# Transposing by VectorE blocks and a round trip through DRAM in place of TensorE, in a two-layer hybrid network

## The chip, the cores and the metric

The kernel runs on one core of a Trainium2 chip. The metric is the device time of one execution in microseconds (us). A core has five engines with a program each: TensorE (PE in the rows, its weight loads PEld), VectorE (DVE), ScalarE (ACT), GpSimd (POOL) and SyncE (SP). They run side by side and wait for one another by semaphores; each takes its instructions in the order in which they stand. TensorE ran at the full granted clock, 1.00 (2.4 GHz), throughout the profiled execution.

## The reference

Sequence of 256 tokens, width 2048, two layers, everything float32. Cut to what matters:

```
layer 0: x = x + dilated_attention(x)   # 16 heads of 128; q, k RMS-normed; softmax over three patterns; @ w_o
         x = x + conv_ffn(x)            # (silu(conv(h @ w_up)[gate]) * conv(..)[up]) @ w_down, inner width 5632
layer 1: x = x + mlstm_mixer(x)         # 4 heads, q/k of 256, v and output gate of 512; gated scan; @ w_out
         x = x + conv_ffn(x)
```

## The kernel before

Every product with a weight matrix is float32 made from two float32r parts. ACT copies a piece of a weight tile to the high part `wh` (L105), DVE subtracts to get the low part `wl` (L107). Activations have a high and a low half too (`xs`, `HID`). Three products are summed: high x high, high x low weight, low activation x high weight.

All weight tiles run through one list of *parts* of at most 1024 columns. A loop at the end of the kernel takes part j: it loads and splits it (`load_split`), and emits the products of part j - 2 (`AHEAD = 2`). Buffers: four for `wst` (the raw tile), three each for `wh` and `wl`. Work that belongs between parts is hung up with `at(j, f)`, to stand just ahead of the products of part j, or is called from the last part's `post`. The tile framework then orders each engine's program and sets the semaphores; it may move such work back when it reckons its inputs to come late.

Two kinds of product:

- *stationary-x* (`mm_b`): 128 tokens of x are stationary, 512 weight columns stream. Used for query, key and value, and for the mixer's value and output gate. A chunk of 512 output columns has eight parts of 12 matmuls. In the first four parts of the program `late=True` puts all products with `wl` last; otherwise, for each weight row block, high, low and low-activation products alternate (L207, L208, L209).
- *stationary-w* (`mm_t`): 128 weight columns are stationary, the 512 columns [high | low] of the activation stream. `wide` is the product with `wh`, `narrow` the one with `wl` (256 columns). Used for the FFN, both output projections and the mixer's query and key.

The attention comes first: eight chunks q, k, q, k, ... of four heads, and then four chunks of values. Of a chunk come the RMS norm of each head (`qk_post`: squares on ACT, the power -0.5 on POOL at L149, scaling on DVE at L310), and then transposes on TensorE, which bring [token, channel] to [channel, token] in PSUM, copied out by ACT (`qk_transpose`, L320 and L324). Scores, softmax (`scores`) and the transposes of the probabilities (`p_transpose`, L355 and L357) follow, one head a part. `pv` multiplies with the values. In the mixer, the gated output of a head is transposed in the same way (`hs_transpose`, L661), and `gate_weights` spreads the running maximum of the gates over partitions with a float32 matmul (L574).

Of the kernel before, what the change touches and what calls it, by code (L numbers as in the profile page):

```python
# [9 lines left out]
F32 = mybir.dt.float32  # L10
# [62 lines left out]
def hybrid_kernel(ctx: ExitStack, tc: tile.TileContext, x, small, negT, sel, g_attn, gain, w_qkv, w_o, w_gates, w_qk, w_vo,  # L73
# [6 lines left out]
    work = ctx.enter_context(tc.tile_pool(name="work", bufs=2))  # L80
    psum = ctx.enter_context(tc.tile_pool(name="psum", bufs=4, space=PSUM))


# [89 lines left out]

    def mm_t(acc, wh, wl, base, ks, xs, first, last):
# [13 lines left out]

        for step in ((narrow, wide) if last else (wide, narrow)):
            step()  # L190

    def mm_b(accs, wh, wl, ks, xs, first, last, n=512, late=False):

        if late:
            order = [(xp, wp, i, tt) for xp, wp in ((0, wh), (S, wh), (0, wl)) for i in range(len(ks)) for tt in range(NT)]
            for xp, w, i, tt in order:
                nc.tensor.matmul(accs[tt], xs[ks[i]][:, xp + tt * P:xp + (tt + 1) * P], w[:, i * n:(i + 1) * n],
                                 start=first and xp == 0 and w is wh and i == 0, stop=False)
            return
        for i, k in enumerate(ks):  # L200
            h = wh[:, i * n:(i + 1) * n]
            lo = wl[:, i * n:(i + 1) * n]
            for tt in range(NT):
                xh = xs[k][:, tt * P:(tt + 1) * P]
                xl = xs[k][:, S + tt * P:S + (tt + 1) * P]
                a = accs[tt]
                nc.tensor.matmul(a, xh, h, start=first and i == 0, stop=False)  # L207
                nc.tensor.matmul(a, xh, lo, start=False, stop=False)  # L208
                nc.tensor.matmul(a, xl, h, start=False, stop=last and i == len(ks) - 1)  # L209

# [35 lines left out]


    st = {}

# [23 lines left out]

    def b_chunk(src, xs_of, post, opening=False):

        hold = {}

        def mm(wh, wl, q):
            if q == 0:
                hold["a"] = [acc_tile(f"accb{tt}") for tt in range(NT)]  # L280
            mm_b(hold["a"], wh, wl, (2 * q, 2 * q + 1), xs_of(), q == 0, q == 7, late=opening and q < 4)
# [31 lines left out]

    def qk_transpose(which, g):
        raw = st.pop(("raw", which, g))
        for a in range(0, GRP, 2):
            pt = psum.tile([P, 512], F32, name="ptq", tag="m")
            for b in range(2):
                for tt in range(NT):
                    nc.tensor.transpose(pt[:, b * S + tt * P:b * S + (tt + 1) * P],  # L320
                                        raw[:, tt, (a + b) * P:(a + b + 1) * P], ident)
            slot = ((0, 1, 20), (2, 3, 21))[which][(g * 2 + a // 2) % 3]
            t = work.tile([P, 512], F32, name=f"qkT{which}", tag=f"hid{slot}", bufs=1)
            nc.scalar.activation(t, pt, AF.Copy, scale=C("qk_gain")[:, which:which + 1])  # L324
            for b in range(2):
                qkT[which, g * GRP + a + b] = t[:, b * S:(b + 1) * S]
# [23 lines left out]

    def p_transpose(h):
        p = SMX.pop(h)
        pp = psum.tile([P, 512], F32, name="ppt", tag="m")
        for b in range(3):
            nc.tensor.transpose(pp[:, b * P:(b + 1) * P], p[:, b * P:(b + 1) * P], ident)  # L355
# [19 lines left out]
    def pv(h):  # L375
        v = st["v", h // GRP]
        a = (h % GRP) * P
        t = PT.pop(h)
        po = psum.tile([P, 512], F32, name="po", tag="m")
        nc.tensor.matmul(po[:, :P], v[:, 0, a:a + P], t[:, :P], start=True, stop=True)  # L380
        nc.tensor.matmul(po[:, P:S], v[:, 0, a:a + P], t[:, P:S], start=True, stop=False)  # L381
        nc.tensor.matmul(po[:, P:S], v[:, 1, a:a + P], t[:, S:384], start=False, stop=True)  # L382
# [7 lines left out]
    def attn_units():  # L390
        for c in range(8):
            g, which = c // 2, c % 2
            post = qk_post(which, g)
            if c == 0:

                j = b_chunk([w_qkv[c, q] for q in range(4)], lambda: st["xs"], lambda accs: st.update(first=accs),
                            opening=True)
                at(12, lambda post=post: post(st.pop("first")))
                at(j + 9, lambda: qk_transpose(0, 0))
# [107 lines left out]
    def gate_product():  # L507
        xs = st["xs"]
        pg = psum.tile([P, 512], F32, name="pg", tag="m")
        for k in range(KT):  # L510
            nc.tensor.matmul(pg[:16], st["gw"][:, k], xs[k], start=k == 0, stop=k == KT - 1)  # L511
        st["sel"] = work.tile([P, LH * P], F32, name="sel", tag="hid21", bufs=1)
        nc.sync.dma_start(st["sel"], sel)
        st["negT"] = work.tile([P, 384], F32, name="negT", tag="hid20", bufs=1)
# [53 lines left out]

    def gate_weights():
        (F, c), M = st["gF"], st["gM"]  # L570
        args = []
        for h in range(LH):
            pm = psum.tile([P, 512], F32, name="pm", tag="m")
            nc.tensor.matmul(pm[:, :S], st["sel"][:LH, h * P:(h + 1) * P], M, start=True, stop=True)  # L574
            ar = work.tile([P, 384], F32, name=f"ar{h}", tag=f"hid{16 + h}", bufs=1)
            nc.vector.tensor_tensor(ar[:, :S], pm[:, :S], st["negT"][:, :S], op=ALU.add)
            nc.vector.tensor_tensor(ar[:, S:], pm[:, P:S], st["negT"][:, S:], op=ALU.add)
            for tt, sl in ((0, slice(0, S)), (1, slice(S, 384))):
                nc.scalar.activation(ar[:, sl], ar[:, sl], AF.Exp, bias=c[:, tt, h:h + 1])
            args.append(ar)  # L580
        pmc = psum.tile([P, 512], F32, name="pmc", tag="m")
# [4 lines left out]
        nc.scalar.activation(en, en, AF.Exp, scale=-1.0)  # L586
        st["E"], st["en"] = args, en

# [67 lines left out]
    def hs_transpose(h):  # L656
        o = st.pop(("hs", h))
        for a in range(4):
# [6 lines left out]
            HID[4 * h + a] = t  # L665

    def lstm_units():
        for n in range(KT):
            which, h, i = n // 8, (n % 8) // 2, n % 2

            def post(acc, n=n, which=which, h=h, i=i):
# [3 lines left out]
                LQ[which, h, i] = t  # L675
            side = {0: gate_product, 2: gate_logs, 4: gate_sums, 6: gate_max, 9: gate_weights}.get(n)

# [5 lines left out]
        for h in range(LH):  # L683
# [4 lines left out]
            if h < LH - 1:  # L688
                at(j + 2, lambda h=h: hs_transpose(h))

# [107 lines left out]
```

## Time and profile before

| | us |
|---|---|
| median of 3 runs (lowest, highest) | 2257.88 (2257.12, 2258.18) |
| profiled execution: its own time | 2257.33 |
| its span on the core | 2255.5 |
| TensorE busy in the span | 2249.5 |
| VectorE busy | 1572.6 |
| ScalarE busy | 1224.4 |
| GpSimd busy | 20.1 |

The times of the rows are those of the profiled execution. A matmul's row gives its duration with fill and drain, so durations of neighbours overlap; what a matmul costs on TensorE is the distance between starts. DVE and ACT instructions overlap a little at their starts as well. In a group row, what follows the bar is busy time in total, mean duration in ns, then the engine's idle time just ahead and what ended it.

### The profile page before, as it was taken

To read this page: it belongs to the slowest core of one execution; us is meant where nothing else is said; L and a number is where in the kernel's file an instruction comes from. 1 tells how busy PE (TensorE), PEld (TensorE's weight loads), DVE (VectorE), ACT (ScalarE), POOL (GpSimd) and SP (SyncE) were. 2 spreads that over 40 slices of the span, in tenths; PEclk is the share of its full clock that TensorE was granted. 3 is DMA by queue.
4 is the path that set the end of the run, shared out by engine and by line. 5 is a ranking of instruction groups with operands and counts; after the bars stand their busy time and mean duration, and the time that the engine had idled before them with its cause. 6 is when DMAs were issued, how large, how long until landed. Compare 5 with 4: busy or idle time off the path is not lost.

```text
span 2255.5 us, 31873 instructions
## 1 busy us (share of the span) xinstructions
PE 2249.5 (100%) x12370; PEld 1948.0 (86%) x12370; DVE 1572.6 (70%) x2522; ACT 1224.4 (54%) x1878; POOL 20.1 (1%) x20
## 2 busy tenths in 40 slices
PE   9999999999999999999999999999999999999999
PEld 7888888888888888888888887888888888888888
DVE  6666566777865688876677555667888656788755
ACT  6666445555644555565556444456665445566543
POOL 0000000000000000000000000000000000000000
PEclk9999999999999999999999999999999999999999
DMA  7544445555545655545555454455554556555464
GB/s 296 181 168 168 166 171 187 187 188 189 191 162 191 219 187 187 188 164 188 208 177 187 173 182 176 174 190 186 193 192 176 169 191 213 189 191 192 166 202 144
DMA packets 67399, 419.90 MB, mean 186 GB/s; under 512 B 7600, under 2 KB 9904, under 8 KB 28592
## 3 DMA queue, kind: packets, MB, share of 16 engines
q1 hardware_dynamic: 64800, 415.76, 52.7%
q8 instruction: 97, 1.59, 0.3%
q10 hardware_dynamic: 2448, 2.11, 0.3%
q14 instruction: 54, 0.44, 0.1%
HBM read 415.74 MB, written 2.10 MB: 185 GB/s over the span
## 4 chain that ended last, share of the span: by engine, by line
PE 99%; DVE 0%; DMA 0%; issue 0%; ACT 0%; SPq 0%; DVEq 0%; ACTq 0%
PE acct L181 51%; PE acct L186 26%; PE accb L208 6%; PE accb L209 6%; PE accb L207 6%; PE pn L611 0%; PE ptq L320 0%; PE psc L332 0%; DMA wst<-in_w_qkv 0%; PE ppt L355 0%; PE pg L511 0%; PE po L381 0%; PE po L382 0%; PE po L380 0%; PE psc L331 0%; PE pth L661 0%
## 5 line engine op out<-in xcount | busy, mean ns | idle before, releaser
L107 DVE TENSOR_TENSOR wl<-wst,wh 128x1024 fp32r<-128x1024 f32 (+1 forms) x864 | 972.1, 1126 | 327.6 <-ACT wh L105 315.7
L105 ACT ACTIVATE wh<-wst 128x1024 fp32r<-128x1024 f32 (+1 forms) x864 | 844.3, 977 | 552.2 <-PE acct L181 342.8
L181 PE MATMUL acct<-xs,wh 128*128 128x512 f32 x3072 | 736.7, 391 | 0.0
L181 PEld LDWEIGHTS acct<-xs,wh 128*128 128x128 f32 x3072 | 563.9, 188 | 109.4 <-issue 0.3
L181 PE MATMUL acct<-hid,wh 128*128 128x512 f32 x1920 | 483.9, 394 | 0.0
L186 PEld LDWEIGHTS acct<-xs,wl 128*128 128x128 f32 x3072 | 393.9, 191 | 15.0
L181 PEld LDWEIGHTS acct<-hid,wh 128*128 128x128 f32 x1920 | 344.2, 188 | 64.8
L186 PE MATMUL acct<-xs,wl 128*128 128x256 f32 x3072 | 398.5, 283 | 0.0
L186 PEld LDWEIGHTS acct<-hid,wl 128*128 128x128 f32 x1920 | 256.8, 188 | 21.2 <-ACT hid L384 0.2
L186 PE MATMUL acct<-hid,wl 128*128 128x256 f32 x1920 | 261.5, 279 | 0.0
L207 PE MATMUL accb<-wh,xs 128*128 128x512 f32 x624 | 249.7, 400 | 0.1
L208 PE MATMUL accb<-wl,xs 128*128 128x512 f32 x624 | 243.4, 390 | 0.5 <-DVE wl L107 0.5
L209 PE MATMUL accb<-wh,xs 128*128 128x512 f32 x624 | 243.5, 390 | 0.0
L209 PEld LDWEIGHTS accb<-wh,xs 128*128 128x128 f32 x624 | 117.1, 188 | 24.9
L208 PEld LDWEIGHTS accb<-wl,xs 128*128 128x128 f32 x624 | 117.3, 188 | 24.1 <-DVE wl L107 1.0
L207 PEld LDWEIGHTS accb<-wh,xs 128*128 128x128 f32 x624 | 117.2, 188 | 23.6 <-ACT wh L105 0.6
L474 ACT ACTIVATE hid<-pr 128x256 fp32r<-128x256 f32 x88 | 36.7, 418 | 176.2 <-DVE pr L472 176.2
L240 DVE TENSOR_TENSOR uz<-acct,ev 128x256 f32<-128x256 f32 x88 | 37.4, 425 | 123.6 <-ACT ev L238 123.6
L238 ACT ACTIVATE ev<-acct 128x256 f32<-128x256 f32 x192 | 73.8, 385 | 75.8 <-PE acct L181 66.5
L468 ACT ACTIVATE sg<-gy 128x256 f32<-128x256 f32 x88 | 36.8, 418 | 142.3 <-DVE gy L456 142.3
L456 DVE SCALAR_TENSOR_TENSOR gy<-gz,sm,gy 128x255 f32<-128x255 f32 (+2 forms) x224 | 106.7, 478 | 2.3 <-ACT gy L452 1.7
L244 DVE TENSOR_TENSOR xT<-acct,xT 128x256 f32<-128x256 f32 x96 | 40.8, 425 | 96.4 <-PE acct L181 96.1
(144 smaller groups left out, 998.9 us busy)
## 6 DMA issues: line engine op xcount, KB each, us to landing
wst<-in_w_up SPq DMA_DIRECT2D x176, 1024.0 KB, 4.8
wst<-in_w_down SPq DMA_DIRECT2D x128, 704.0 KB, 4.1
wst<-in_w_qkv SPq DMA_DIRECT2D x46, 1024.0 KB, 4.8
wst<-in_w_vo SPq DMA_DIRECT2D x32, 1024.0 KB, 4.8
wst<-in_w_o SPq DMA_DIRECT2D x16, 1024.0 KB, 4.7
wst<-in_w_qk SPq DMA_DIRECT2D x16, 1024.0 KB, 4.8
wst<-in_w_out SPq DMA_DIRECT2D x16, 1024.0 KB, 4.7
xT<-in_x SPq DMA_DIRECT2D x8, 256.0 KB, 8.2
```

The costliest lines, as they stand in the source:

```text
L105: nc.scalar.activation(wh[:, :n], w, AF.Copy)
L107: nc.vector.tensor_tensor(wl[:, :n], w, wh[:, :n].bitcast(F32), op=ALU.subtract)
L181: nc.tensor.matmul(acc, wh[:, (base + i) * P:(base + i + 1) * P], xs[k], start=first and i == 0, stop=last and i == n - 1)
L186: nc.tensor.matmul(acc[:, :S], wl[:, (base + i) * P:(base + i + 1) * P], xs[k][:, :S], start=False, stop=False)
L207: nc.tensor.matmul(a, xh, h, start=first and i == 0, stop=False)
L208: nc.tensor.matmul(a, xh, lo, start=False, stop=False)
L209: nc.tensor.matmul(a, xl, h, start=False, stop=last and i == len(ks) - 1)
L238: nc.scalar.activation(t, acc[:, S:], AF.Copy)
L240: nc.vector.tensor_tensor(z, acc[:, :S], t, op=ALU.add)
L244: nc.vector.tensor_tensor(xT[k], acc[:, :S], xT[k], op=ALU.add)
L456: nc.vector.scalar_tensor_tensor(y[:, d:], z[:, :S - d], w, y[:, d:], op0=ALU.mult, op1=ALU.add)
L468: nc.scalar.activation(g, y, AF.Silu)
```

## The change

1. The transposes of query, key and probabilities, and of three of the four mixer heads, leave TensorE. DVE transposes blocks of 32x32 in place of that (`turn_blocks`), four transfers on POOL's queue write the four partition groups into a DRAM tile, each so that the block column becomes the partition, and one more fetches it back (`fetch_blocks`). ACT (and DVE for the mixer's low half) then reads the fetched tile where it read PSUM. A probability tile is fetched straight into `PT`.
2. The work is hung up at other parts: a chunk is turned 4 parts behind its end and taken 5 parts later; scores come at j + 10, 12, 14, 16 (before j + 7 to 10) and the probabilities' turns 4 parts behind each.
3. `mm_b` always has the products with `wl` last.
4. The second of four parts in the down projection has `narrow` ahead of `wide` (`turn`).
5. `gate_weights` works with two float32r halves of the maximum, one head in each of four units, and `sel` is loaded by POOL with a cast.

```diff
-    def mm_b(accs, wh, wl, ks, xs, first, last, n=512, late=False):
...
+    def mm_b(accs, wh, wl, ks, xs, first, last, n=512):
+
+        for xp, w in ((0, wh), (S, wh), (0, wl)):
+            for i, k in enumerate(ks):
+                for tt in range(NT):
+                    nc.tensor.matmul(accs[tt], xs[k][:, xp + tt * P:xp + (tt + 1) * P], w[:, i * n:(i + 1) * n],
...
+    def turn_blocks(srcs, tag, bufs):
...
+        t = work.tile([P, 4, m, n, 32], F32, name="tb", tag=tag, bufs=bufs)
+        for u, src in enumerate(srcs):
+            nc.vector.transpose(t[:, :, :, u].rearrange("p j m r -> p m j r"),
+                                src.rearrange("p (m j r) -> p m j r", m=m, j=4))
+        d = dram.tile([4, 32, 4, run], F32, name=f"d{run}", tag=f"d{run}")
+        for i in range(4):
+            nc.gpsimd.dma_start(d[:, :, i].rearrange("j c x -> c j x"),
+                                t[32 * i:32 * (i + 1)].rearrange("p j m n r -> p j (m n r)"))
+        return d
+
+    def fetch_blocks(d, dst):
+        nc.gpsimd.dma_start(dst, d.rearrange("j c i x -> (j c) (i x)"))
...
-        for step in ((narrow, wide) if last else (wide, narrow)):
+        for step in ((narrow, wide) if last or turn else (wide, narrow)):
...
+    def qk_turn(which, g):
+        raw = st.pop(("raw", which, g))
+        d = turn_blocks([raw[:, tt] for tt in range(NT)], "tok", 4)
+        t = work.tile([P, 1024], F32, name="td", tag="tok", bufs=4)
+        fetch_blocks(d, t)
+        st["td", which, g] = t
...
+    def p_turn(h):
+        d = turn_blocks([SMX.pop(h)], "y", 3)
         t = work.tile([P, 384], F32, name=f"PT{h}", tag=f"hid{h + 4}", bufs=1)
-        nc.scalar.activation(t, pp[:, :384], AF.Copy)
-        PT[h] = t
+        fetch_blocks(d, t)
...
-                at(j + 5, lambda which=which, g=g: qk_transpose(which, g))
+                at(j + 4, lambda which=which, g=g: qk_turn(which, g))
+                at(j + 9, lambda which=which, g=g: qk_take(which, g))
             if which == 1:
                 for a in range(GRP):
-                    at(j + 7 + a, lambda h=g * GRP + a: scores(h))
-                    at(j + 11 + a, lambda h=g * GRP + a: p_transpose(h))
+                    at(j + 10 + 2 * a, lambda h=g * GRP + a: scores(h))
+                    at(j + 14 + 2 * a, lambda h=g * GRP + a: p_turn(h))
...
+        for i in range(2):
+            nc.tensor.matmul(pm[:, :S], st["sel"][:LH, h * P:(h + 1) * P], m2[:, i], start=i == 0, stop=i == 1)
...
-                at(j + 2, lambda h=h: hs_transpose(h))
+                at(j + 2, lambda h=h: hs_turn(h))
+                at(j + 7, lambda h=h: hs_take(h))
```

TensorE's order at the scores of the third head group, before (`psc` are scores, `accb` the running chunk, `ptq` and `ppt` transposes; this is the fourth score of the group):

```order
L207 MATMUL accb1_1713<-wh_1591,xs1_97 128x512
L208 MATMUL accb1_1713<-wl_1593,xs1_97 128x512
L209 MATMUL accb1_1713<-wh_1591,xs1_97 128x512
L331 MATMUL psc_1730<-qkT1_1559,qkT0_1376 128x128
L332 MATMUL psc_1730<-qkT1_1559,qkT0_1376 128x256
L207 MATMUL accb0_1712<-wh_1626,xs2_107 128x512
L208 MATMUL accb0_1712<-wl_1628,xs2_107 128x512
```

and now, three scores of that group (the first was named for 4.7 parts earlier):

```order
L199 MATMUL accb0_1681<-wh_1748,xs11_200 128x512
L199 MATMUL accb1_1682<-wh_1748,xs11_200 128x512
L346 MATMUL psc_1699<-qkT1_1677,qkT0_1481 128x128
L347 MATMUL psc_1699<-qkT1_1677,qkT0_1481 128x256
L346 MATMUL psc_1752<-qkT1_1677,qkT0_1481 128x128
L347 MATMUL psc_1752<-qkT1_1677,qkT0_1481 128x256
L346 MATMUL psc_1824<-qkT1_1679,qkT0_1483 128x128
L347 MATMUL psc_1824<-qkT1_1679,qkT0_1483 128x256
L199 MATMUL accb0_1681<-wl_1750,xs10_197 128x512
```

Scores that stood one a part stand three in a row, inside a part.

VectorE's order in the same place, before (from the second head's maxima to the next `wl`; 12 rows stand between two of them at most):

```order
L340 TENSOR_REDUCE mx_1635<-sc_1633 128x1 x2
L341 TENSOR_SCALAR mx_1635<-mx_1635 128x2
L334 TENSOR_TENSOR sc_1696<-psc_1693,sm_68 128x384
L344 SCALAR_TENSOR_TENSOR p_1638,den_1636<-e_1637,sm_68 128x128
L340 TENSOR_REDUCE mx_1698<-sc_1696 128x1 x2
L344 SCALAR_TENSOR_TENSOR p_1638,den_1636<-e_1637,sm_68 128x256
L341 TENSOR_SCALAR mx_1698<-mx_1698 128x2
L346 RECIPROCAL den_1636<-den_1636 128x2
L348 TENSOR_SCALAR p_1638<-p_1638,den_1636 128x128
L348 TENSOR_SCALAR p_1638<-p_1638,den_1636 128x256
L107 TENSOR_TENSOR wl_1691<-wst_1687,wh_1689 128x1024
```

and now, the last rows of 26 between two low parts (`tb` is the block-transposed tile):

```order
L248 STREAM_TRANSPOSE tb_1771<-raw_1647 128x4x4x32
L359 SCALAR_TENSOR_TENSOR p_1760,den_1758<-e_1759,sm_70 128x128
L248 STREAM_TRANSPOSE tb_1771<-raw_1647 128x4x4x32
L359 SCALAR_TENSOR_TENSOR p_1760,den_1758<-e_1759,sm_70 128x256
L248 STREAM_TRANSPOSE tb_1815<-p_1707 128x3x4x32
L361 RECIPROCAL den_1758<-den_1758 128x2
L355 TENSOR_REDUCE mx_1829<-sc_1827 128x1
L363 TENSOR_SCALAR p_1760<-p_1760,den_1758 128x128
L363 TENSOR_SCALAR p_1760<-p_1760,den_1758 128x256
L355 TENSOR_REDUCE mx_1829<-sc_1827 128x1
L108 TENSOR_TENSOR wl_1859<-wst_1855,wh_1857 128x1024
```

The next low part now stands behind two heads, the scaling of a query chunk and three block transposes.

GpSimd's order over the attention, before, is powers alone:

```order
L149 ISA
L149 TENSOR_TENSOR rcol<-ir,mhalf 128x4
L149 TENSOR_TENSOR qf<-ir,mhalf 128x8 x8
L149 TENSOR_TENSOR rcol<-ir,mhalf 128x4 x2
L149 TENSOR_TENSOR lf_11863<-ir,mhalf 128x2
```

and now, from the power of a key chunk to that of the next query chunk (`d` are DRAM tiles, `td` and `PT` fetched ones):

```order
L150 TENSOR_TENSOR qf_1463<-ir_1464,mhalf_72 128x8
L252 DMA d96_1505<-tb_1503 32x4x96 x2
L257 DMA PT5_1417<-d96_1412 128x384
L252 DMA d96_1505<-tb_1503 32x4x96 x2
L252 DMA d96_1548<-tb_1546 32x4x96 x2
L257 DMA PT6_1510<-d96_1505 128x384
L252 DMA d96_1548<-tb_1546 32x4x96 x2
L252 DMA d256_1558<-tb_1555 32x4x256 x2
L257 DMA PT7_1553<-d96_1548 128x384
L252 DMA d256_1558<-tb_1555 32x4x256 x2
L257 DMA td_1563<-d256_1558 128x1024
L150 TENSOR_TENSOR qf_1658<-ir_1659,mhalf_72 128x8
```

A fetch waits for its four writes, and what stands behind it on the queue waits with it, the next power included.

## Rows read from the trace of the kernel before

**Rows 1.** The page, engines: busy us (share of span) x instructions.
```profile
PE 2249.5 (100%) x12370; PEld 1948.0 (86%) x12370; DVE 1572.6 (70%) x2522; ACT 1224.4 (54%) x1878; POOL 20.1 (1%) x20
```
**Rows 2.** The page, chain that ended last, share by engine.
```profile
PE 99%; DVE 0%; DMA 0%; issue 0%; ACT 0%; SPq 0%; DVEq 0%; ACTq 0%
```
**Rows 3.** PE timeline at a query chunk's transposes: start us, duration us, instruction.
```profile
114.03 0.39 PE L209 MATMUL accb<-wh,xs 128*128 128x512 f32 x1
114.26 1.03 PE L320 MATMUL ptq<-sm,raw 128*128 128x128 f32 x8
...
115.36 0.39 PE L208 MATMUL accb<-wl,xs 128*128 128x512 f32 x1
```
**Rows 4.** PE timeline at a probability tile's transposes.
```profile
133.97 0.40 PE L209 MATMUL accb<-wh,xs 128*128 128x512 f32 x1
134.21 0.49 PE L355 MATMUL ppt<-sm,p 128*128 128x128 f32 x3
...
134.78 0.39 PE L208 MATMUL accb<-wl,xs 128*128 128x512 f32 x1
```
**Rows 5.** Windows, one head group: all engines; then DVE at L107, at L310.
```profile
71.50:121.00 49.50, 49.50 (x237) 41.31 (x237) 31.98 (x79) 31.12 (x69) 3.28 (x2) 1.00 0.50 170
...
71.50:121.00 49.50, 19.44 (x16) 1.00 0.50 170
...
71.50:121.00 49.50, 3.32 (x16) 1.00 0.50 170
```
**Rows 6.** Groups of instructions: the three kinds of transposes on PE.
```profile
L320 PE MATMUL ptq<-sm,raw 128*128 128x128 f32 x64 | 8.3, 272 | 0.0
...
L355 PE MATMUL ppt<-sm,p 128*128 128x128 f32 x48 | 7.8, 272 | 0.0
...
L661 PE MATMUL pth<-sm,osb 128*128 128x128 f32 x32 | 4.1, 272 | 0.0
```
**Rows 7.** PE timeline at the float32 gate matmuls, and a row of 256-column passes.
```profile
1193.42 1.99 PE L574 MATMUL pm<-cm,sel 4*128 4x256 f32 x8
1195.34 0.50 PE L181 MATMUL acct<-xs,wh 128*128 128x512 f32 x1
...
1197.68 1.60 PE L186 MATMUL acct<-xs,wl 128*128 128x256 f32 x12
```
**Rows 8.** PE timeline near the start.
```profile
20.15 0.50 PE L208 MATMUL accb<-wl,xs 128*128 128x512 f32 x1 [0.53 <-DVE wl L107]
```
**Rows 9.** Waits: us in total, times, longest us.
```profile
ACT wh L105 <- PE acct L181: 342.8, 259, 2.7
```
**Rows 10.** Groups of instructions: DVE, 512 and 384 elements.
```profile
L334 DVE TENSOR_TENSOR sc<-psc,sm 128x384 f32<-128x384 f32 x16 | 8.9, 555 | 4.7 <-PE psc L332 4.7
...
L652 DVE TENSOR_TENSOR osb<-osb,num 128x512 f32<-128x512 f32 x8 | 5.4, 692 | 2.1 <-ACT osb L651 2.1
```
**Rows 11.** PE timeline at a score.
```profile
120.37 0.39 PE L209 MATMUL accb<-wh,xs 128*128 128x512 f32 x1
120.60 0.38 PE L331 MATMUL psc<-qkT,qkT 128*128 128x128 f32 x2
...
121.49 0.40 PE L208 MATMUL accb<-wl,xs 128*128 128x512 f32 x1
```
**Rows 12.** POOL timeline, its first two powers.
```profile
39.67 1.01 POOL L149 TENSOR_TENSOR rcol<-ir,mhalf 128x4 f32<-128x4 f32 x1 [39.23 <-DVE ir L148]
48.06 1.64 POOL L149 TENSOR_TENSOR qf<-ir,mhalf 128x8 f32<-128x8 f32 x1 [7.37 <-DVE ir L148]
```
**Rows 13.** SP timeline: an issue of a transfer.
```profile
5.77 0.33 SPq L102 DMA_DIRECT2D wst<-in_w_qkv  x1
```
**Rows 14.** DMA issues: transfers, KB each, median us from issue to landing.
```profile
wst<-in_w_down SPq DMA_DIRECT2D x128, 704.0 KB, 4.1
...
out<-xT ACTq DMA_DIRECT2D x16, 128.0 KB, 2.9
```
**Rows 15.** Windows, attention's first stretch (columns as in rows 5).
```profile
22.00:71.50 49.50, 49.50 (x231) 41.23 (x230) 30.45 (x53) 32.27 (x70) 4.29 (x3) 1.00 0.64 240
```
**Rows 16.** DVE timeline at the first power on POOL.
```profile
40.19 1.23 DVE L107 TENSOR_TENSOR wl<-wst,wh 128x1024 fp32r<-128x1024 f32 x1 [0.59 <-ACT wh L105]
```

More of the change, by code (lines that the diff above doesn't have):

```diff
@@ L171, in row_factor, with mm_t @@
         st["row"] = r
-    def mm_t(acc, wh, wl, base, ks, xs, first, last):
+    def mm_t(acc, wh, wl, base, ks, xs, first, last, turn=False):
         n = len(ks)
@@ L187, in narrow @@
                                  start=False, stop=False)
-        for step in ((narrow, wide) if last else (wide, narrow)):
+        for step in ((narrow, wide) if last or turn else (wide, narrow)):
             step()
-    def mm_b(accs, wh, wl, ks, xs, first, last, n=512, late=False):
[L194 to L209, printed above, removed]
+    def mm_b(accs, wh, wl, ks, xs, first, last, n=512):
[3 more added lines that the diff above has]
+                    nc.tensor.matmul(accs[tt], xs[k][:, xp + tt * P:xp + (tt + 1) * P], w[:, i * n:(i + 1) * n],
+                                     start=first and xp == 0 and w is wh and i == 0,
+                                     stop=last and w is wl and i == len(ks) - 1)
     def t_unit(src, ks, operand, post, split=None):
@@ L280, in mm @@
                 hold["a"] = [acc_tile(f"accb{tt}") for tt in range(NT)]
-            mm_b(hold["a"], wh, wl, (2 * q, 2 * q + 1), xs_of(), q == 0, q == 7, late=opening and q < 4)
+            mm_b(hold["a"], wh, wl, (2 * q, 2 * q + 1), xs_of(), q == 0, q == 7)
             if q == 7:
@@ L312, in qk_post, with qk_take @@
         return post
-    def qk_transpose(which, g):
+    def qk_turn(which, g):
         raw = st.pop(("raw", which, g))
-        for a in range(0, GRP, 2):
[L317 to L321, printed above, removed]
+        d = turn_blocks([raw[:, tt] for tt in range(NT)], "tok", 4)
+        t = work.tile([P, 1024], F32, name="td", tag="tok", bufs=4)
+        fetch_blocks(d, t)
+        st["td", which, g] = t
+    def qk_take(which, g):
+        v = st.pop(("td", which, g)).rearrange("p (i m r) -> p m i r", i=4, r=32)
+        for a in range(0, GRP, 2):
             slot = ((0, 1, 20), (2, 3, 21))[which][(g * 2 + a // 2) % 3]
             t = work.tile([P, 512], F32, name=f"qkT{which}", tag=f"hid{slot}", bufs=1)
-            nc.scalar.activation(t, pt, AF.Copy, scale=C("qk_gain")[:, which:which + 1])
+            nc.scalar.activation(t.rearrange("p (m i r) -> p m i r", m=4, i=4), v[:, 2 * a:2 * a + 4], AF.Copy,
+                                 scale=C("qk_gain")[:, which:which + 1])
             for b in range(2):
@@ L349, in scores @@
         SMX[h] = p
[L351 to L355, printed above, removed]
+    def p_turn(h):
+        d = turn_blocks([SMX.pop(h)], "y", 3)
         t = work.tile([P, 384], F32, name=f"PT{h}", tag=f"hid{h + 4}", bufs=1)
-        nc.scalar.activation(t, pp[:, :384], AF.Copy)
-        PT[h] = t
+        fetch_blocks(d, t)
+        PT[h] = t.rearrange("p (i b r) -> p b i r", i=4, r=32)
     def v_post(g):
@@ L567, in gate_max, with gate_split, gate_weights @@
         st["gM"] = ab[cur]
[L569 to L580, printed above, removed]
+    def gate_split():
+        M = st["gM"]
+        m2 = work.tile([LH, 2, S], F32R, name="m2", tag="hid15", bufs=1)
+        nc.scalar.activation(m2[:, 0], M, AF.Copy)
+        nc.vector.tensor_tensor(m2[:, 1], M, m2[:, 0].bitcast(F32), op=ALU.subtract)
+        st["m2"] = m2
+    def gate_weights(h):
+        (F, c), M, m2 = st["gF"], st["gM"], st["m2"]
+        pm = psum.tile([P, 512], F32, name="pm", tag="m")
+        for i in range(2):
+            nc.tensor.matmul(pm[:, :S], st["sel"][:LH, h * P:(h + 1) * P], m2[:, i], start=i == 0, stop=i == 1)
+        ar = work.tile([P, 384], F32, name=f"ar{h}", tag=f"hid{16 + h}", bufs=1)
+        nc.vector.tensor_tensor(ar[:, :S], pm[:, :S], st["negT"][:, :S], op=ALU.add)
+        nc.vector.tensor_tensor(ar[:, S:], pm[:, P:S], st["negT"][:, S:], op=ALU.add)
+        for tt, sl in ((0, slice(0, S)), (1, slice(S, 384))):
+            nc.scalar.activation(ar[:, sl], ar[:, sl], AF.Exp, bias=c[:, tt, h:h + 1])
+        st.setdefault("E", []).append(ar)
+        if h < LH - 1:
+            return
         pmc = psum.tile([P, 512], F32, name="pmc", tag="m")
@@ L586, in gate_weights @@
         nc.scalar.activation(en, en, AF.Exp, scale=-1.0)
-        st["E"], st["en"] = args, en
+        st["en"] = en
     def lstm_w(h):
@@ L665, in hs_transpose, with hs_turn, hs_take @@
             HID[4 * h + a] = t
+    def hs_turn(h):
+        o = st.pop(("hs", h))
+        d = turn_blocks([o[:, tt] for tt in range(NT)], "tok", 4)
+        t = work.tile([P, 1024], F32, name="td", tag="tok", bufs=4)
+        fetch_blocks(d, t)
+        st["td", h] = t
+    def hs_take(h):
+        v = st.pop(("td", h)).rearrange("p (i a t r) -> p a t i r", i=4, a=4, r=32)
+        for a in range(4):
+            t = hid_tile(4 * h + a)
+            hi = t[:, :S].rearrange("p (t i r) -> p t i r", t=NT, i=4)
+            nc.scalar.activation(hi, v[:, a], AF.Copy)
+            nc.vector.tensor_tensor(t[:, S:].rearrange("p (t i r) -> p t i r", t=NT, i=4), v[:, a], hi.bitcast(F32),
+                                    op=ALU.subtract)
+            HID[4 * h + a] = t
     def lstm_units():
@@ L675, in post @@
                 LQ[which, h, i] = t
-            side = {0: gate_product, 2: gate_logs, 4: gate_sums, 6: gate_max, 9: gate_weights}.get(n)
+            side = {0: gate_product, 2: gate_logs, 4: gate_sums, 6: gate_max, 8: gate_split,
+                    **{9 + h: lambda h=h: gate_weights(h) for h in range(LH)}}.get(n)
             def finish(acc, post=post, n=n, side=side):
```

24 lines of the change are left out of this document (14 added, 10 removed).

## Prediction

> **What bounds the kernel now.** I read the page first. TensorE (PE) is busy through the whole span, 2249.5 of 2255.5 us [rows 1], and the chain that ended last is PE for 99% of it [rows 2]. So an instruction on PE costs its slot, and work elsewhere costs nothing until it makes PE wait. VectorE (DVE) is busy for 70%, ScalarE (ACT) for 54%, GpSimd (POOL) for 1% [rows 1]: the change takes slots from PE and loads DVE and POOL.
>
> Second, the PE timeline around the removed work. A wide matmul starts 0.23 us after the one ahead. Around the eight transposes of a query or key chunk, the start of the last matmul ahead (114.03) and of the second one behind (115.36) lie 1.33 us apart where two slots take 0.45: the block costs 0.88 us [rows 3]. The same reading of the three transposes of a probability tile gives 0.81 less 0.46, that is 0.35 us [rows 4].
>
> Third, the windows. One head group (a query and a key chunk, four softmax tiles) takes 49.5 us of PE. In it DVE is busy 31.98 us, 19.44 of them with the low parts wl and 3.32 with scaling the query and key rows; that leaves 9.22, 2.3 us a head, for the softmax [rows 5]. The DMA engines are at a share of 0.50 with 170 GB/s.
>
> **The change, part by part.** *Transposes leave PE.* Rows count 64 matmuls for query and key, eight blocks of eight; 48 for probabilities, 16 blocks of three; 32 for the mixer, four blocks of eight, of which one stays [rows 6]. 8 x 0.88 + 16 x 0.35 + 3 x 0.88 = 15.3 us, all on the path.
>
> *Forget-gate matrix.* Before, eight float32 passes stand on PE from 1193.42 to 1195.34: 1.92 us. After, there are eight passes of 256 columns in float32r, the kind whose twelve take 1.60 us in the row below, hence 8 x 0.12 = 0.96 [rows 7]. Saved: 1.0 us.
>
> *Low parts last.* The one wait for wl in stationary-x products is at 20.15 us: 0.53 us idle [rows 8]. Asked for eight matmuls (1.8 us) later it is gone: 0.5 us. The order of the products does not change their number or width. In the down projection, second part, the low product now goes first, so wl is wanted up to 1.2 us earlier (five wide slots). I cost it at nothing: ACT waits 342.8 us in all for PE to give back weight buffers [rows 9], so wh, and wl behind it, are made two parts ahead. Without that cover it would be 64 x 1.2 = 77 us at worst.
>
> The gain is 15.3 + 1.0 + 0.5 = 16.8 us.
>
> *DVE.* A group gets four block transposes of 128x512 and four of 128x384. No row shows this operation; for 512 elements from SBUF to SBUF the nearest two rows are 0.69 us, for 384 it is 0.55 [rows 10]; bounds are nothing, since no row excludes a far quicker one, and 1.23 us, a low part of 1024 elements [rows 16]. I take the near rows: 4 x 0.69 + 4 x 0.55 = 5.0 us, so DVE has 37.0 us in a group that is now 49.5 - 2 x 0.88 - 4 x 0.35 = 46.3 us long. On average there is room. At 1.23 us apiece it would be 41.8, still under; at nothing PE gains only the loss that follows.
>
> It is not even, though. In the order of the third group the first three scores stand together on PE, and DVE has 26 rows between two low parts: two whole heads (4.6), the sum and maxima of a third (about half a head's 2.3, 1.1), eight scalings (half of the 3.32, 1.7), three block transposes (1.9, less 0.2 for starts that overlap), then the low part (1.2): 10.3 us, with a power on POOL in between that DVE waits for, 1.64 us [rows 12], and an estimated 0.3 for the exponentials: 12.2. PE has, from the first score's end, 36 slots of 0.23 us and three more scores at 0.66 (121.49 less 120.37, less two slots [rows 11]): 8.2 + 2.0 = 10.2 us. Loss: 2.0 us, once. In the other groups at most two scores stand together, or no scaling falls in between; I charge nothing there. Bounds: 0 and 4 x 2.0.
>
> *POOL.* This is the disputed term. A group issues 2 x 5 + 4 x 5 = 30 transfers from POOL, beside two powers (3.3 us). The trace has no DMA from POOL. The lower bound of one issue is 0.33 us, what an SP issue takes [rows 13]; the upper is 2.9 us, if POOL is held until a transfer of 128 KB to HBM has landed [rows 14]. Between ends that far apart I take 1.0 us, the row of POOL's own short work on 128 partitions x 4 elements [rows 12], since each write here also has 32 partitions x 4 runs. Then POOL has 33.3 us in 46.3. Two of four issues of the next transfer stand ahead of each fetch in the order, so of the 2.9 us to landing 0.9 is waited for: six fetches, 5.4 us, sum 38.7. POOL keeps up. The break-even: 30g + 3.3 + 6 x (2.9 - 2g) = 46.3 gives g = 1.43 us.
>
> *The wait that is added.* The scores wait for ACT's copy of the fetched tile. The path is two block transposes (1.3), four issues (4.0), the rest of the landing (1.9), the fetch of 512 KB (3.5, between 2.9 for 128 KB and 4.1 for 704 KB [rows 14]), ACT 0.7: 11.4 us, and five parts of 2.73 us (13.7) lie between turn and take. What stands ahead in POOL's queue eats the 2.3 that are left, which is why the order has the scores later. Behind the waiting copy on ACT stand wh parts, and behind a late power on DVE the wl parts; PE waits for both. I charge one exposed landing, 2.9 us, over all groups; bounds 0 and four times that. The three mixer heads have no such reader: their tiles are read in the output product alone.
>
> *DMA engines.* Out and back, the tiles add 8 x 1.0 + 16 x 0.4 + 3 x 1.0 = 17.4 MB, 14.4 of them in some 230 us of attention: 63 GB/s, by the share of 0.50 at 170 GB/s about 0.19 more, 0.69. The first stretch of the attention ran at 0.64 and 240 GB/s [rows 15] with PE busy throughout. No cost.
>
> Sum: 16.8 - 2.0 - 2.9 = 11.9 us off the profiled execution. That took 2257.33 us (span and 1.8 us around it), 0.55 us under the median of the three runs, 2257.88. Forecast: 2245.4 us.
>
> **The rivals.** A difference under 0.2%, 4.5 us, can't be told from no change here.
>
> *POOL partly late, gain given back.* With g between 1.25 and 1.5 us each group waits some 3 us at its scores: 4 x 3 = 12 us beside the 2.0: 2257.3 - 16.8 + 2.0 + 12 = 2254.5. For it: in the order the scores of the third group stand 4.7 parts behind the place that the code names, as if POOL's queue were expected to lag. Against: POOL has 46 us for 30 short issues.
>
> *POOL sets the pace (the other side).* One mechanism: its in-order queue of issues and waits is longer than the group. At g = 1.64 us (the longer power [rows 12]) a group needs 30 x 1.64 + 3.3 = 52.5 us, 6.2 more than PE; four groups, 25 us: 2257.3 - 16.8 + 2.0 + 25 = 2267. At 2.0 us it is 68 us and 2310; at the upper bound 2.9, 176 us and 2418. It makes the kernel slower by more than 4.5 us from g = 1.6 on. For it: no row excludes it, and DVE's scaling stands behind POOL's power, so a late POOL holds wl too. The Trainium skill, in DMA: Bandwidth & Descriptors, section Anatomy of one DMA, gives about 2.0 us and bytes over 436 GB/s for a transfer from this queue; were POOL held for all of that (2.3 us for 128 KB) the time would be about 2347 by it, an estimate. No row here tells a queue's hold from a landing on POOL.
>
> *DVE and POOL block each other.* If POOL's building of a transfer holds an SBUF port that a low part (two SBUF inputs) needs, each of 30 issues costs DVE up to 1.0 us: 37 + 30 = 67 us in a group of 46.3, 4 x 20.7 = 83 us: 2257.3 - 16.8 + 83 = 2323. Against it stands one row: the low part that starts at 40.19, while POOL's power runs from 39.67 to 40.68 [rows 12], takes 1.23 us [rows 16], as in the group 19.44 / 16 = 1.22 [rows 5]. That is the rule of the Trainium skill in SBUF — State Buffer, section Who interferes with whom (a Vector instruction with two SBUF inputs shuts out, and is shut out by, a GpSimd one that reads SBUF); this one row doesn't agree, though the power reads little. What building a transfer reads, no row shows.
>
> *That the change doesn't do what it says* I leave out: the order of the changed program has no transpose of these tiles on PE.
>
> **How the numbers follow.** The forecast 0.55 (its own range 2240 to 2253: all covers hold, or both losses double); gain given back 0.16 (2253 to 2262); POOL sets the pace 0.22 (2262 to 2420, most of it below 2290, since one issue of 1.6 to 1.8 us is nearer to POOL's rows than 2.9); the port 0.07. That is faster 0.55, same 0.16, slower 0.29. The range 2239 to 2288 leaves out 0.04 below and some 0.14 above.
>
> **What would show it.** PE rows for query, key and probability transposes gone, 32 less 24 left for the mixer; block transposes near 0.7 and 0.55 us; PE idle of about 2 us ahead of a wl in the third group (about 195 us), and little ahead of the scores. POOL busy or issuing for some 33 us in a group. The forecast is wrong if PE idles more than 3 us at each group's first score, with ACT's copy of td as the releaser and POOL's transfers behind it, or if low parts grow beyond 1.23 us in the attention.

## The result, and the profile after

The changed kernel takes 2271.60 us (median; 2267.69 to 2273.33) against 2258.03 in the same runs: ratio 1.0057, 95% interval 1.0045 to 1.0068. It is slower by 0.6%. The forecast, 11.9 us faster, was wrong in its direction. The profiled execution took 2267.69 us; it is the quickest of four, and the account below is of it alone (the others show a mean granted clock of 0.995 or 0.996 beside its 0.997, and of them there is no trace).

The page's engine line shows the transposes gone from PE, 136 matmuls fewer than in [rows 1], and PE no longer busy throughout (busy us, share, instructions):

```profile
PE 2239.2 (99%) x12234; PEld 1936.2 (85%) x12234; DVE 1589.5 (70%) x2561; ACT 1225.8 (54%) x1869; POOL 96.4 (4%) x156
```

The waits of PE, which in the attention were one of 0.5 us before [rows 8] (engine, line, releaser: us in total, times, longest):

```profile
PE psc L346 <- ACT qkT L338: 13.0, 4, 4.7
PE accb L199 <- DVE wl L108: 5.1, 3, 2.8
PE accb L199 <- ACT wh L106: 3.0, 1, 3.0
```

That is 21.1 us in eight waits. The timeline of the first two shows the chain (start, duration, instruction, in brackets the idle time ahead of it and its releaser):

```profile
48.65 0.17 DVE L318 TENSOR_SCALAR qf<-qf 128x8 f32<-128x8 f32 x1 [1.75 <-POOL qf L150]
...
51.56 1.29 DVE L248 STREAM_TRANSPOSE tb<-raw 128x512 f32<-128x512 f32 x2
...
68.95 0.72 ACT L338 ACTIVATE qkT<-td,sm 128x512 f32<-128x512 f32 x1 [7.84 <-DMA td<-d]
...
69.87 1.04 ACT L106 ACTIVATE wh<-wst 128x1024 fp32r<-128x1024 f32 x1
...
70.97 2.11 PE L199 MATMUL accb<-wh,xs 128*128 128x512 f32 x8 [3.04 <-ACT wh L106]
...
76.11 1.29 DVE L248 STREAM_TRANSPOSE tb<-raw 128x512 f32<-128x512 f32 x2
77.33 4.59 DVE L108 TENSOR_TENSOR wl<-wst,wh 128x1024 fp32r<-128x1024 f32 x4
...
78.57 1.20 PE L199 MATMUL accb<-wl,xs 128*128 128x512 f32 x4 [2.78 <-DVE wl L108]
```

ACT stands 7.84 us at the copy of the first query tile. The weight part queued behind the copy is late for PE by 3.04 us; DVE, which had waited for that part, then scales and turns the next chunk ahead of its backlog of four low parts, and PE waits once more. The copy comes up in ACT's order at 61.1, 9.6 us after the turn began at 51.56. It waits because its fetch left late (POOL, same stretch):

```profile
53.17 2.36 POOL L252 DMA_DIRECT2D d<-tb  x4 [4.56 <-DVE tb L248]
62.01 0.58 POOL L257 DMA_DIRECT2D td<-d  x1 [6.48 <-DMA d<-tb]
```

The four writes are issued in 2.4 us. POOL then waits 6.48 us for them to land, and the fetch takes 6.9 more (62.01 to 68.95). The windows say what else was under way (length, busy of PE, PEld, DVE, ACT, POOL, granted clock, DMA share, GB/s); the first two are from this trip, the last three stand at three of the waits:

```profile
55.50:58.50 3.00, 3.00 (x15) 2.47 (x14) 2.17 (x2) 2.32 (x5) 0.03 (x1) 1.00 0.87 257
62.50:65.00 2.50, 2.50 (x12) 2.07 (x12) 0.00 (x0) 0.00 (x0) 0.09 (x1) 1.00 0.94 364
79.94:83.35 3.41, 3.41 (x10) 2.63 (x9) 1.98 (x2) 0.40 (x1) 0.00 (x0) 0.50 0.94 263
93.59:97.00 3.41, 3.41 (x10) 2.74 (x9) 2.94 (x7) 2.18 (x9) 0.37 (x1) 0.50 0.00 0
257.43:260.84 3.41, 3.14 (x12) 2.96 (x13) 1.42 (x4) 1.77 (x3) 0.00 (x0) 0.50 0.00 0
```

While the writes and then the fetch were out, the DMA engines ran at shares of 0.87 and 0.94: they were moving weight loads (of 4.3 MB between 50 and 65 us, 3.7 are the SP queue's). The last three rows are a second price. With waits of 2.8, 4.0 and 4.7 us (ending at 78.57, 92.64 and 257.70) the granted clock is 0.50 (1.2 GHz) for 3.41 us each: half the work of PE's busy time in them, 5.0 us.

The account closes: 2257.3 - 15.2 (transposes) - 0.5 (the early wait) + 21.1 + 5.0 = 2267.7, measured 2267.7. PE's busy time says the same: it fell by 10.3 us, which is 15.2 less 5.0 to within 0.1.

### The profile page after: what moved, and what is told of

It reads as the page before. It is cut to its first block, busy times and chain, and to the rows that moved or that the text cites. A ratio compares the mean times of both kernels' runs of the same rounds, so it can differ in the third digit from the quotient of the medians.

```text
span 2265.9 us, 32014 instructions
## 1 busy us (share of the span) xinstructions
PE 2239.2 (99%) x12234; PEld 1936.2 (85%) x12234; DVE 1589.5 (70%) x2561; ACT 1225.8 (54%) x1869; POOL 96.4 (4%) x156
## 4 chain that ended last, share of the span: by engine, by line
PE 88%; issue 0%; DMA 0%; DVE 0%; ACT 0%; POOLq 0%
PE acct L183 51%; PE acct L188 26%; PE accb L199 10%; PE pn L633 0%; DMA td<-d 0%; PE po L392 0%; PE po L394 0%; PE po L393 0%; PE pg L524 0%; PE pls L615 0%; PE psc L347 0%; PE pls L618 0%; PE pm L594 0%; PE psc L346 0%; PE pd L634 0%
## 5 line engine op out<-in xcount | busy, mean ns | idle before, releaser
L183 PE MATMUL acct<-hid,wh 128*128 128x512 f32 x1920 | 473.2, 394 | 0.0
L183 PEld LDWEIGHTS acct<-hid,wh 128*128 128x128 f32 x1920 | 349.1, 188 | 69.8
L188 PEld LDWEIGHTS acct<-xs,wl 128*128 128x128 f32 x3072 | 394.0, 191 | 15.1
L199 PE MATMUL accb<-wh,xs 128*128 128x512 f32 x1280 | 323.1, 394 | 3.2 <-ACT wh L106 3.0
L199 PEld LDWEIGHTS accb<-wh,xs 128*128 128x128 f32 x1280 | 239.9, 189 | 54.1 <-ACT wh L106 4.8
L188 PEld LDWEIGHTS acct<-hid,wl 128*128 128x128 f32 x1920 | 247.1, 188 | 15.3 <-ACT hid L396 0.2
L188 PE MATMUL acct<-hid,wl 128*128 128x256 f32 x1920 | 250.7, 279 | 0.0
L199 PE MATMUL accb<-wl,xs 128*128 128x512 f32 x640 | 172.9, 392 | 5.1 <-DVE wl L108 5.1
L469 DVE SCALAR_TENSOR_TENSOR uy<-uz,sm,uy 128x255 f32<-128x255 f32 (+1 forms) x176 | 84.1, 478 | 0.1
L488 DVE TENSOR_TENSOR hid<-pr,hid 128x256 fp32r<-128x256 f32 x88 | 37.4, 424 | 39.7 <-ACT hid L487 39.7
```

The costliest lines, as they stand in the source:

```text
L199: nc.tensor.matmul(accs[tt], xs[k][:, xp + tt * P:xp + (tt + 1) * P], w[:, i * n:(i + 1) * n], start=first and xp == 0 and w is wh and i == 0,
L469: nc.vector.scalar_tensor_tensor(y[:, d:], z[:, :S - d], w, y[:, d:], op0=ALU.mult, op1=ALU.add)
L488: nc.vector.tensor_tensor(o[:, S:], pr, o[:, :S].bitcast(F32), op=ALU.subtract)
```

## The experiments

**Three parts later.** `pinned` gives an instruction a fixed place in its engine's order, behind the last one that the program names ahead of it, without a wait; and all are named three parts later:

```diff
-                at(j + 9, lambda which=which, g=g: qk_take(which, g))
+                at(j + 12, lambda which=which, g=g: pinned(mybir.EngineType.Activation, lambda: qk_take(which, g)))
...
-                    at(j + 10 + 2 * a, lambda h=g * GRP + a: scores(h))
-                    at(j + 14 + 2 * a, lambda h=g * GRP + a: p_turn(h))
+                    at(j + 13 + 2 * a, lambda h=g * GRP + a: pinned(mybir.EngineType.PE, lambda: scores(h)))
+                    at(j + 17 + 2 * a, lambda h=g * GRP + a: p_turn(h))
...
-                    at(j + 2 + a, lambda h=g * GRP + a: pv(h))
+                    at(j + 12 - 4 * g + a, lambda h=g * GRP + a: pv(h))
```

> ACT's copies of the fetched query and key tiles, the scores and the turns of the probabilities come three parts (8.2 us) later than in the changed kernel, each held at its place behind the weight part that stands ahead of it; the products with the values move back with them. Theory A (the round trip through DRAM lands later than the five parts given to it, and ACT, DVE and then PE stand behind the waiting copy): in the changed kernel's trace that copy waits 7.8, 4.1, 1.1, 3.3 and 6.5 us where PE stalls; three parts cover all of these, so the 21 us of PE waits in the attention fall under 5 and the time comes to 2243 to 2249 us. Rival B (POOL's queue of issues sets the pace): the same issues stand in the same queue, each group is as long as before, and the time stays at 2266 to 2273 us.

2242.42 us, ratio 0.9938 (0.9925 to 0.9951): faster than both kernels, and 0.6 us under A's range. On the first trip the landings are as long as in the changed kernel (POOL), but ACT comes to the copy after them, with no idle time ahead of it:

```profile
53.55 2.36 POOL L257 DMA_DIRECT2D d<-tb  x4 [4.56 <-DVE tb L253]
62.35 0.57 POOL L262 DMA_DIRECT2D td<-d  x1 [6.44 <-DMA d<-tb]
```
```profile
70.15 1.06 ACT L106 ACTIVATE wh<-wst 128x1024 fp32r<-128x1024 f32 x1 [1.66 <-PE accb L204]
71.11 1.32 ACT L343 ACTIVATE qkT<-td,sm 128x512 f32<-128x512 f32 x2
```

PE's waits in the attention:

```profile
PE psc L351 <- ACT qkT L343: 1.6, 1, 1.6
...
PE accb L204 <- DVE wl L108: 0.5, 2, 0.4
PE accb L204 <- ACT wh L106: 0.2, 1, 0.2
```

2.3 us in place of 21.1, and no stretch at half clock in the attention. B falls. How the later groups got there, the table behind the last run shows: not by later copies.

**No weight loads.** `if 4 <= u < 48: pass` ahead of the load of unit u, which keeps one of the first four tiles.

> From the fifth load of the first query chunk on, the attention's weight loads (44 loads of 1 MB) are left out, so its products use wrong weights; everything else and the order of instructions on ACT is that of the changed kernel. Theory A1 (a transfer of POOL's waits on the DMA engines behind a weight load): the writes, 4.8 us from issue to landing in the changed kernel, and the fetches of 512 KB, 4.7 us, fall to 3 us or less, PE's waits in the attention fall from 21 us under 7, time 2244 to 2251 us. Rival A2 (the transfers themselves take that long, by their short runs or by their queue): landings stay at 4.3 to 4.8 us, PE's waits above 15 us, time 2262 to 2273 us.

2241.82 us, 0.9931 (0.9917 to 0.9944). That is 2.2 us under A1's range. PE waits 1.4 us in the attention. DMA issues of the changed kernel (transfer, count, KB, median us to landing), then of this one:

```profile
d<-tb POOLq DMA_DIRECT2D x44, 128.0 KB, 4.8
td<-d POOLq DMA_DIRECT2D x11, 512.0 KB, 4.7
d<-tb POOLq DMA_DIRECT2D x64, 48.0 KB, 4.3
PT<-d POOLq DMA_DIRECT2D x16, 192.0 KB, 4.2
```
```profile
d<-tb POOLq DMA_DIRECT2D x44, 128.0 KB, 2.7
td<-d POOLq DMA_DIRECT2D x11, 512.0 KB, 3.8
d<-tb POOLq DMA_DIRECT2D x64, 48.0 KB, 2.1
PT<-d POOLq DMA_DIRECT2D x16, 192.0 KB, 2.7
```

The same transfers from the same queue, in the same order on ACT, land 1.5 to 2.2 us sooner when no weights move (medians; the large fetch 0.9: the eight of the attention took 3.5 to 3.9 us, not 3 as expected, where they had taken 3.9 to 7.6). So the weight loads lengthen the landings, and A2 falls; that a transfer stands *behind* a load, as A1 has it, no row shows. The Trainium skill, in DMA: Bandwidth & Descriptors, section Queues, rings and completion order, says that a DMA engine serves its queues in turn but finishes a whole packet of descriptors of one before it goes on. That would make a small transfer wait behind large ones as seen; the packets themselves no row here shows.

**Probabilities and mixer alone.** `qk_turn` and `qk_take` replaced by the old `qk_transpose`, scores at j + 7 + a, turns at j + 11 + a.

> Query and key are transposed on PE at the places of the kernel before, and the scores stand at their old places; the probabilities and three mixer heads go by DVE blocks and DRAM, each turned four parts behind its scores. Theory A: a fetched probability tile is read by nothing before the products with the values, tens of us later, so no instruction queues behind a landing; gain 16 x 0.34 + 3 x 0.89 us and about 0.2 for the rest, no PE wait over 1 us: 2248 to 2251 us. Rival C (block transposes and issues themselves hold up DVE or its port): the gain is lost, 2255 us or more, with PE waiting for low parts.

2248.27 us, 0.9958 (0.9945 to 0.9972). Waits in the attention:

```profile
PE accb L199 <- ACT wh L106: 0.4, 1, 0.4
PE ptq L332 <- DVE raw L322: 0.4, 1, 0.4
```

A holds; a landing that nothing waits for costs nothing. C falls.

**All transposes on PE.** The three old functions back, the rest of the change kept.

> All transposes stay on PE at the places of the kernel before; what is left of the change is the order with low parts last, the low product first in the second quarter of the down projection, and the two float32r halves in the gate matrix. By the changed kernel's trace the four gate products cost 0.63 us each (2.5 in all) where the eight float32 passes cost 2.2, and the one wait for a low part near the start (0.5 us) is gone: 2257 to 2259 us, no change that can be told. Rival D (low parts last lets the weight parts run late somewhere): 2262 us or more, with PE waiting for wl or wh outside the attention too.

2256.30 us, 0.9993 (0.9984 to 1.0002), 0.7 us under the range: no difference that can be told. What the remaining edits are worth lies between 3.6 us of gain and 0.5 of loss; neither help nor harm is shown. D falls.

**Later, but not held.** The three-part run without `pinned`.

> As the run with everything three parts later, but ACT's copies are not held at their places: the scores stand at the same places on PE as there, while in ACT's order the copies of the fetched tiles stand 4, 1, 3, 2, 3, 2, 3 and 2 weight parts further ahead. Theory A (what costs is the copy that waits in ACT's queue, with the weight parts behind it): ACT waits again for fetched tiles, PE for wh, wl and scores with 5 to 20 us in all, 2246 to 2262 us. Rival F (what counts is that the scores stand later on PE): as the held run, 2240 to 2245 us.

2262.43 us (1.0023; 1.0011 to 1.0034), 0.4 us above A's range. PE's scores stand where they stand in the held run; ACT's copies stand one to four weight parts earlier:

```profile
PE accb L199 <- ACT wh L106: 7.8, 5, 3.5
PE psc L346 <- ACT qkT L338: 6.0, 3, 3.0
PE accb L199 <- DVE wl L108: 2.1, 3, 1.3
```

These 15.9 us, and 20 us of time, hang on the place of eight pairs of copies in ACT's queue. F falls. It is the cleanest pair of runs here: PE's whole order and the loads' are the same, and DVE's and POOL's shift only a little with the copies. It also shows that the part named in `at` is not the place in the program: the first copy stood behind the same weight part of ACT's order, the 22nd, with or without the three parts, until it was held.

**Held, nothing later.** The control: `pinned` and the moved `pv`, offsets of the changed kernel.

> The control of the run with everything three parts later: its two other edits alone, the copies and scores held at the places that the code names and the products with the values moved back; nothing comes later than in the changed kernel. Theory A: the landing is still later than five parts, PE waits 18 us or more in the attention, 2262 to 2273 us. Rival G (holding the order or moving the value products was the cure, not the three parts): 2240 to 2250 us.

2269.62 us (1.0052), 20.6 us of PE waits. G falls: without the later offsets the other two edits cure nothing. The planner did not keep the named places even so: each group's first score stands where the changed kernel has it, to 0.2 of a part.

**Query and key alone.** `p_turn` replaced by the old `p_transpose`.

> The probabilities are transposed on PE, four parts behind their scores; query, key and three mixer heads go by DVE blocks and DRAM as in the changed kernel. Theory A: the waiting copies are those of query and key, so 15 to 25 us of PE waits stay, with some us for a slower clock behind them, against a gain of 8 x 0.88 + 3 x 0.89 + 0.2 = 9.9 us: 2262 to 2274 us. Rival H (the probability tiles' 80 transfers stand ahead of query's and key's on POOL's queue and make them late): without them the copies find their tiles, 2248 to 2253 us.

2278.77 us (1.0094; 1.0079 to 1.0109), 4.8 us above A's range. PE waits 22.6 us, and the clock is at 0.50 in five stretches, three of them twice as long as before; the first two:

```profile
71.31:74.72 3.41, 3.41 (x10) 2.65 (x9) 1.22 (x4) 3.34 (x8) 1.66 (x1) 0.50 0.00 0
91.79:98.60 6.81, 5.93 (x16) 4.90 (x17) 3.01 (x7) 4.36 (x13) 1.08 (x1) 0.50 0.08 12
```

H's forecast fails, but the time does not settle H, since the planner moved something else as well: without the probabilities' transfers it placed the key copies of groups two to four three to six weight parts earlier on ACT. The trips settle it. In the changed kernel those key chunks had their four writes between those of the probabilities. In the last group the turn began at 231.53, and the fourth write was issued 13.9 us later:

```profile
231.53 1.29 DVE L248 STREAM_TRANSPOSE tb<-raw 128x512 f32<-128x512 f32 x2
...
232.06 2.18 POOL L252 DMA_DIRECT2D d<-tb  x4
236.82 0.56 POOL L257 DMA_DIRECT2D PT<-d  x1 [2.58 <-DMA d<-tb]
237.36 2.18 POOL L252 DMA_DIRECT2D d<-tb  x4
244.33 0.56 POOL L257 DMA_DIRECT2D PT<-d  x1 [4.79 <-DMA d<-tb]
244.88 1.10 POOL L252 DMA_DIRECT2D d<-tb  x2
252.22 0.56 POOL L257 DMA_DIRECT2D td<-d  x1 [6.24 <-DMA d<-tb]
```

POOL is not busy there but waiting, with others' writes behind a fetch that waits for its own. The fetches of the three later key chunks left 17.0, 17.5 and 20.7 us after the turn in the changed kernel, and 8.9, 11.2 and 10.9 in this run. So H holds for the length of these trips; that the gain did not show is the work of the earlier copies.

**Weight loads in halves.** `load_split(j < 96, ...)` in place of `j < 4`.

> The changed kernel with the attention's 1 MB weight loads cut in two of 512 KB each, issued a part apart; the bytes are the same. Theory A1 in its narrow form (a POOL transfer stands behind one weight load on the DMA engines, so a shorter load ahead is a shorter wait): landings of query and key writes fall from 4.8 towards 3.5 to 4.2 us, PE's waits from 21 to 8 to 17 us, 2252 to 2266 us. Rival A1' (it stands behind whatever bytes are under way, in loads of any size): landings within 0.3 us of the changed kernel's and 2265 to 2273 us.

2272.07 us (1.0066; 1.0049 to 1.0083), PE waits 19.5 us, query and key writes land in 4.4 us (changed kernel 4.8). The narrow form falls: time and waits lie above its ranges, the time in that of A1'. The landing lies between the two expectations, 0.1 us short of A1', but the runs with whole loads have 4.1 to 4.8 as well. So the size of one load, between 0.5 and 1 MB, is not what counts here; that the bytes under way are, is argued.

**One part later, held.**

> As the run with everything three parts later and held, but one part (2.7 us) later. Theory A: one part covers the third wait of the changed kernel's copies (1.1 us) and nearly the fourth (3.3), and leaves 5.1, 1.4 and 3.8 us of the others at ACT; PE's waits fall from 21 us to between 5 and 14, some of it paid twice where the clock falls: 2247 to 2261 us, between the changed kernel and the three-part run. Rival F' (any later place frees the order, by a step and not by degrees): 2240 to 2246 us.

2271.16 us (1.0056; 1.0043 to 1.0070): a miss for both. The four waits at the scores grew:

```profile
PE psc L351 <- ACT qkT L343: 23.0, 4, 8.5
```

The expectation counted from the places that the code names. In the changed kernel the planner had pushed groups two to four further back than named (their first scores stand at parts 44.5, 61.7 and 79.0 of PE's order); with the offsets of this run it placed them at 42, 58 and 74, earlier than in the changed kernel. Against the built order it is a run with less time for the key trips (11.8 us in place of 18 to 20), and it waits more, as A has it.

**Four parts later, held.**

> The same, four parts (10.9 us) later. Theory A: the three-part run has 2.3 us of PE waits left in the attention; one more part takes most of these and nothing else changes: 2239.5 to 2243.5 us, not told apart from three parts. Rival I (later scores press softmax, probability turns and value products against the end of the attention, or tiles wait for their buffers): over 2246 us.

2244.29 us, 0.9937 (0.9923 to 0.9950), beside 0.9938 with three parts: not told apart, though 0.8 us above A's range, since the waits did not shrink. PE waits 3.6 us in the attention, 2.6 of them for wl. I falls.

**The trips side by side.** For each trip, what it takes (from its first block transpose on DVE to the landing of its fetch) and what it is given (from the same start until ACT comes to the copy), in us, for the first query chunk and for the key chunks of groups two to four:

| run | first: takes / given | keys: take | keys: given |
|---|---|---|---|
| changed kernel | 17.4 / 9.6 | 21.0, 21.5, 25.4 | 19.9, 18.3, 18.9 |
| held, nothing later | 17.2 / 11.7 | 24.6, 21.8, 20.9 | 17.7, 18.4, 19.0 |
| one part | 17.4 / 13.8 | 20.9, 19.8, 16.1 | 11.8, 11.9, 11.8 |
| three parts, held | 17.5 / 19.2 | 18.0, 15.4, 15.5 | 18.1, 15.3, 15.3 |
| three parts, not held | 17.8 / 9.6 | 17.1, 19.0, 18.2 | 10.2, 10.6, 10.0 |
| query and key alone | 17.1 / 9.6 | 14.1, 16.2, 15.3 | 10.7, 10.7, 9.7 |
| no weight loads | 10.3 / 9.6 | 15.2, 15.1, 14.7 | 18.8, 19.1, 18.9 |

Where a trip takes more than it is given, ACT waits for the difference; PE then loses some or all of it. The first trip was cured by time, since its copy moved back. The later key trips were not: in the three-part run their copies stand one to three weight parts *earlier* than in the changed kernel. There the probabilities' turns moved, the key fetches left 8.7, 10.1 and 8.3 us after the turn in place of 17.0 to 20.7, and the trips came to fit to within 0.3 us. The expectation of the three-part run had the time nearly right and half of the reason.

## Why the prediction was wrong, point by point

- *Transposes leave PE: right.* 15.2 us by the same reading of more blocks of the trace before (8 x 0.88 + 16 x 0.34 + 3 x 0.89); the one block that stays in the mixer is there. The gain came in once the waits were gone: the three-part run is 16.0 us faster than before.
- *Gate matrix: wrong by 1.0 us.* Four separate pairs take 0.43 us each from start to next start, 1.7 in all, not 0.96:

```profile
1206.69 0.50 PE L594 MATMUL pm<-m,sel 4*128 4x256 f32 x2
...
1207.12 1.42 PE L183 MATMUL acct<-xs,wh 128*128 128x512 f32 x5
```

  With the slots on both sides a pair costs 0.62, 2.5 in all, where the eight passes cost some 2.2: nothing is saved. A row of twelve in sequence [rows 7] doesn't price two alone.
- *The early wait for wl: right* (none in the waits of after).
- *DVE: right.* The block transposes took what their neighbours in [rows 10] take, and low parts stayed at 1.22 us [rows 5, 16] in the attention after the first group, so the port rival falls. The late low part in the third group cost 1.43 us at 213.69, where 2.0 was forecast:

```profile
L108 DVE TENSOR_TENSOR wl<-wst,wh 128x1024 fp32r<-128x1024 f32 x60 | 72.3, 1217 | 44.2 <-ACT wh L106 39.8 <-PE accb L199 4.4
L248 DVE STREAM_TRANSPOSE tb<-raw 128x512 f32<-128x512 f32 x14 | 9.3, 688 | 0.0
L248 DVE STREAM_TRANSPOSE tb<-p 128x384 f32<-128x384 f32 x13 | 7.4, 567 | 1.4 <-DMA d<-tb 1.4
```

- *POOL's issue: mis-sized, on the safe side.* 0.56 us, not 1.0, nearer to SP's 0.33 [rows 13]; POOL is busy 14 to 20 us in a stretch of 49.5:

```profile
L252 POOL DMA_DIRECT2D d<-tb x108 | 59.7, 558 | 112.2 <-DVE tb L248 88.4 <-DVE p L359 21.2 <-issue 2.6
```

  So the two rivals on POOL's pace fall (they needed 1.25 us and more an issue), though the time given for 1.64 us, 2267, is near the one measured. The time alone would have confirmed the wrong mechanism. What that term had too small is the waiting of fetches for their writes, 0.9 us for each of six, 5.4 in a group: in the third group of the changed kernel it is 19.9 us (POOL's idle time ahead of its fetches), and this made the later key trips long. (The break-even of the same paragraph works out at 1.42 us, not 1.43.)
- *The wait that is added: here the prediction failed.* It priced the way from turn to copy at 11.4 us, 10.7 without ACT's own 0.7, with the landings of [rows 14], put five parts, 13.7 us, between turn and take, and charged one exposed landing of 2.9 us, at most four (11.6). Both sides were off. The first trip took 17.4 us (51.56 to 68.95): the fetch could leave 6.5 us after the end of the last issue, not 1.9, and took 6.9, not 3.5. And it was given 9.6: DVE waited for POOL's power (48.65) and scaled the chunk before it could turn, 4.3 us behind ACT's weight part for the same place (done at 47.2). With 13.7 us the wait would have been 3.7 in place of 7.8. Seven copies waited, 25.3 us of ACT, and PE lost 18.8 us at them or at the weight parts right behind them; the rest of the 21.1 are late low parts, the 1.43 above and one of 0.9.
- *"DMA engines ... No cost": the step behind it.* A share of 0.69 was read as room. PE's loads are two parts ahead and don't mind; a transfer that one instruction waits for does: the engines are at 0.87 and 0.94 in the stretches in which the first trip's transfers were out. Nor does a mean share price a landing. The row of 2.9 us in [rows 14] has the same size, but it comes from ACT's queue, one transfer at a time. Of its 16, 13 ran beside the last down projection's loads at a mean share of 0.62, about that of the changed kernel's attention (0.65), and the last three with hardly a load:

```profile
2137.00:2232.00 95.00, 95.00 (x547) 82.80 (x546) 55.27 (x76) 39.43 (x50) 0.00 (x0) 1.00 0.62 208
...
out<-xT ACTq DMA_DIRECT2D x13, 128.0 KB, 2.9
...
out<-xT ACTq DMA_DIRECT2D x3, 128.0 KB, 1.8
```

  POOL's writes take 2.7 us without loads (second experiment) and 4.8 beside them. Why these lose 2 us and ACT's about 1 stays open: the queue, the number of transfers out at once and the size of the loads differ together, and of the last only a halving was tried.
- *The clock: no term for it.* A wait of PE was priced at its own length; three of the eight cost 1.6 to 1.7 us more each.

## What to carry to other kernels

Before an in-order engine is made to wait for a transfer, price the transfer from rows of the same queue in the same stretch, under the same loads, with what stands ahead of it on that queue. Put the reader behind it by that much in the built order, not in the order that the code names. Where the reader can't be moved, move only those transfers that nothing soon reads: here the probabilities and three mixer heads (with the remaining edits) gave 10 us with no new PE wait over 0.4 us. When a time fits a theory, look whether its own row fits too.

## What was not expected of the hardware

- A transfer of 48 to 192 KB lands in 2.1 to 2.7 us beside no weight loads and in 4.2 to 4.8 beside them, at a mean DMA share of 0.6 to 0.7.
- With waits of PE of 2.8, 4.0 and 4.7 us came 3.4 us each at 1.2 GHz; with one of 3.0 (ending at 70.97) and one of 3.25 (at 201.17) it did not. What tells them apart these runs don't show.
